# Expert stage of a two-layer model: program order on TensorE, nineteen weight places, another order of gathering

## The chip, the cores and the metric

One core of one Trainium2 chip runs the whole kernel. The metric is device microseconds (us) of one execution, the median of several runs. The engines that matter here are TensorE (PE in the profile, its weight loads PEld), VectorE (DVE), ScalarE (ACT), and SyncE (SP), which issues the weight transfers.

## What is computed

The program is a two-layer model on 512 tokens of 1024 features. The change lies in its last part, a mixture of experts. A router gives every token to experts, each of 16 experts takes its first 64 tokens, and each expert is a gated network whose result is added back to the tokens it took, weighted by the router's share:

```python
def expert(x, w_gate, w_up, w_down):          # x: 64 tokens x 1024
    return (silu(x @ w_gate) * (x @ w_up)) @ w_down
```

So 16 experts times three 1024x1024 float32 matrices, 201 MB in all, are read once and used once.

## The kernel before

Function moe (L1495) works on the experts in NB = 8 pairs, the two experts of a pair in the two halves (64 columns each) of the tiles. A matrix of a pair comes as 8 chunks of 1 MB, 192 chunks in all, in the order in which they are used: gate 0, up 0, then for each later pair b gate b, down b-1, up b, and at the end the down matrix of the last pair ("last").

- **Places for weights.** load (L1512) puts chunk n into place n % 17: 8 tiles e_raw, 4 halves of the tiles xh and xl, 2 tiles wraw, and 3 pairs whi and wlo, of an earlier stage. SyncE issues the transfers in this order. Seventeen chunks are asked for before the first product; from then on chunk (L1630) asks for the next one when it is used, and the transfer waits until TensorE has left the place.
- **gather(b)** (L1590). VectorE makes the selection matrix e_oh and its scaled copy e_ohr (L1595, L1598). TensorE multiplies the tokens e_ht by it (L1605) into two PSUM banks "sm" of four blocks each; a block is 128 features, f = 0 to 7, and each is 4 matmuls of the program (8 instructions in the trace). After each two blocks of a bank they are evicted into e_x, the even one by VectorE (L1614), the odd one by ScalarE (L1612). Then come 4 transposes of e_oh (L1618), copied to e_oht (L1620), and 4 small matmuls for the router's shares (L1623, 8 instructions in the trace).
- **product** (L1636) runs over 8 chunks, 4 matmuls of the program to a chunk, 8 in the trace (L1643), into two banks "mm".
- **turn_hidden** (L1647) transposes the hidden values e_hs (L1653) and copies them to e_hid (L1654). **weigh** (L1664) multiplies the down product by the router's shares into e_y. **spread_out** (L1657) multiplies e_y by e_oht (L1661, 2 matmuls for each of 8 blocks t) and VectorE adds the result to the tokens (L1662).
- The loop (from L1671) runs, for each pair b: gate b; the rest of the spreads of b-2 and turn_hidden of b-1; the tanh (L1681, L1682); down b-1 and weigh; gather(b+1); up b; the multiplication by up (L1691); the first spreads of b-1. This is the order in which the program is written. On TensorE the instructions go as a scheduler puts them, by what is ready and by its own estimates, so that pieces of gather(b+1) and of the spreads stand among the matmuls of the products. At the end stand the last product (L1714), finish (L1701) and the normalization of the output.

Of the kernel before, what the change touches and what calls it, by code (L numbers as in the profile page):

```python
# [19 lines left out]
D = 1024  # L20
S = 512
NK = D // 128
NT = S // 128
DFF = 2816
WC = 272
NR = 8


class G:
    pass  # L30


def f32(t):
# [164 lines left out]
def bc(ap, shape):  # L198
    return ap.to_broadcast(shape)
# [64 lines left out]
class Side:  # L264


    def __init__(self):
        self.q = []
# [17 lines left out]
def sm(g):  # L286
    return g.ps_s.tile([128, 512], F32, name="sm")
# [1207 lines left out]
def moe(g, I, P, x_out, out):  # L1495
# [84 lines left out]
    while len(loaded) < NR + 9:  # L1580
        load()
    ye = P.tile([128, 2, D], F32R, name="e_y")
# [4 lines left out]
    xe, oht, hid = {}, {}, {}  # L1587
    pj = [slice(0, 64), slice(64, 128)]

    def gather(b):  # L1590
# [7 lines left out]
        nc.vector.tensor_mul(ohr, oh.rearrange("p i j c -> p i (j c)"), bc(rt[:, :, None], [128, NT, 128]))  # L1598
        xe[b] = P.tile([128, NK, 2, 64], F32, name="e_x", bufs=2)
        for q in range(2):  # L1600
            p = sm(g)
            for k in range(4):
                f = 4 * q + k
                for i in range(NT):
                    nc.tensor.matmul(p[:, k * 128:(k + 1) * 128], ht[:, i, f * 128:(f + 1) * 128], ohr[:, i, :],  # L1605
                                     start=(i == 0), stop=(i == NT - 1))
                if k % 2:
                    for f in (f - 1, f):
                        o = xe[b][:, f].rearrange("p j c -> p (j c)")
                        pk = p[:, (f % 4) * 128:(f % 4 + 1) * 128]  # L1610
                        if f % 2:
                            nc.scalar.activation(o, pk, AF.Identity, scale=w[:, f:f + 1], bias=shift[:, f:f + 1])  # L1612
                        else:
                            nc.vector.tensor_scalar(o, pk, w[:, f:f + 1], shift[:, f:f + 1], op0=OP.mult, op1=OP.add)  # L1614

        p = sm(g)
        for i in range(NT):
            nc.tensor.transpose(p[:, i * 128:(i + 1) * 128], oh[:, i].rearrange("p j c -> p (j c)"), g.ident)  # L1618
        oht[b] = P.tile([128, S], F32R, name="e_oht", bufs=2)
        nc.scalar.copy(oht[b], p)  # L1620
        pa = sm(g)
        for i in range(NT):
            nc.tensor.matmul(pa[:, 0:2], oh[:, i].rearrange("p j c -> p (j c)"), aff[:, i, 2 * b:2 * b + 2],  # L1623
                             start=(i == 0), stop=(i == NT - 1))
        for j in range(2):
            nc.vector.tensor_copy(affs[pj[j], b:b + 1], pa[pj[j], j:j + 1])

    used = [0]

# [3 lines left out]
        used[0] += 1  # L1633
        return loaded[used[0] - 1]

    def product(lhs):  # L1636

        ps = [g.ps_m.tile([128, 512], F32, name="mm") for _ in range(2)]
        for k in range(NK):
            raw = chunk()  # L1640
            for h in range(2):
                for j in range(2):
                    nc.tensor.matmul(ps[h][pj[j], :], lhs(k, j), raw[j][:, h * 512:(h + 1) * 512], start=(k == 0),  # L1643
                                     stop=(k == NK - 1), skip_group_check=True)
        return ps

    def turn_hidden(b, hs):  # L1647

        hid[b] = P.tile([128, NK, 2, 64], F32, name="e_hid")
        for q in range(2):  # L1650
            p = sm(g)
            for k in range(4):
                nc.tensor.transpose(p[:, k * 128:(k + 1) * 128], hs[q][:, k * 128:(k + 1) * 128], g.ident)  # L1653
            (nc.scalar.copy if q else nc.vector.tensor_copy)(  # L1654
                hid[b][:, 4 * q:4 * q + 4].rearrange("p k j c -> p (k j c)"), p)

    def spread_out(b, t):  # L1657

        p = sm(g)
        for s in range(2):  # L1660
            nc.tensor.matmul(p, ye[:, s, t * 128:(t + 1) * 128], oht[b], start=(s == 0), stop=(s == 1))  # L1661
        nc.vector.scalar_tensor_tensor(g.x[t], p, g.mod[:, 40 + t:41 + t], g.x[t], op0=OP.mult, op1=OP.add)  # L1662

    def weigh(b, cols, p):  # L1664

        nc.scalar.activation(ye[:, 0, cols], p, AF.Copy, scale=affs[:, b:b + 1])
        nc.vector.scalar_tensor_tensor(ye[:, 1, cols], p, affs[:, b:b + 1], f32(ye[:, 0, cols]), op0=OP.mult,
                                       op1=OP.subtract)

    gather(0)  # L1670
    for b in range(NB):  # L1671

        pg = product(lambda k, j: xe[b][:, k, j, :])
# [4 lines left out]
        hs = [P.tile([128, 512], F32, name="e_hs", bufs=2) for _ in range(2)]  # L1678
        for h in range(2):
            th = P.tile([128, S], F32, name="e_full", bufs=2)  # L1680
            nc.scalar.activation(th, pg[h], AF.Tanh, scale=0.5)  # L1681
            nc.vector.scalar_tensor_tensor(hs[h], th, 1.0, pg[h], op0=OP.add, op1=OP.mult)  # L1682
        if b:
            ps = product(lambda k, j: hid[b - 1][:, k, j, :])
            for h in range(2):
                weigh(b - 1, slice(h * 512, (h + 1) * 512), ps[h])
        if b + 1 < NB:
            gather(b + 1)
        pu = product(lambda k, j: xe[b][:, k, j, :])
        for h in range(2):  # L1690
            nc.vector.tensor_mul(hs[h], hs[h], pu[h])  # L1691
        if b:
            for t in range(4 if b + 1 < NB else 8):
                spread_out(b - 1, t)
    turn_hidden(b, hs)

    acc, sq = stat_tiles(g)
    last = [P.tile([128, S], F32, name="e_full", bufs=2) for _ in range(2)]
# [10 lines left out]
    for t in range(NK):  # L1709
        raw = chunk()  # L1710
        p = sm(g)
        for k in range(NK):
            for j in range(2):
                nc.tensor.matmul(p[pj[j], 0:128], hid[b][:, k, j, :], raw[j][:, k * 128:(k + 1) * 128],  # L1714
                                 start=(k == 0), stop=(k == NK - 1), skip_group_check=True)
# [333 lines left out]
```

## Time and profile before

| | us |
|---|---|
| median of 3 runs | 3054.05 (3049.53 to 3057.12) |
| the profiled execution | 3055.56 |
| its span | 3053.5 |
| from the first gather matmul (2562.87) to the first matmul of the last product (3013.80) | 450.93 |

Starts in the rows are microseconds from the start of the span. "x48" is a count of instructions; a matmul's duration includes its way through the array, so that consecutive ones overlap. Names like sm<-e_ohr,e_ht are the program's: result, arrow, operands. In brackets stand the idle time of the engine before a row and what ended it.

### The profile page before, as it was taken

The page shows a single profiled execution, that of the slowest core. Times are in us where ns is not written, and L with a number is a line of the kernel's source. Part 1 is how long each engine was busy: PE and PEld are TensorE (multiplying, and loading weights), DVE is VectorE, ACT ScalarE, POOL GpSimd, SP SyncE. Part 2 cuts the span into 40 slices and gives each one's busy share as a digit, 9 for nine tenths or more (in the row PEclk, how much of TensorE's full clock was granted, in tenths as well). Part 3 has the DMA queues.
Part 4 walks back from the last instruction along what each step waited for, and adds up shares of the span by engine and source line. Part 5 has one row for each costly group of instructions (what it writes and reads, how often), then busy time and mean ns, then how long its engine had stood idle before and what let it go on. Part 6 is the DMA issues. An engine that isn't in the chain of part 4 may idle for free. (4 is left out here: it accounts for less than half of the span.)

```text
span 3053.5 us, 37758 instructions
## 1 busy us (share of the span) xinstructions
PE 2905.0 (95%) x15232; PEld 2225.9 (73%) x15232; DVE 1636.6 (54%) x2847; ACT 905.5 (30%) x1515; POOL 321.4 (11%) x260
## 2 busy tenths in 40 slices
PE   7999998999999999999999999999998877999998
PEld 6888887877888888888776788888787765444444
DVE  4445457665444598545676666454765643122213
ACT  3222334543222332223354433222342321010002
POOL 0001012110201102011210201201100110000000
PEclk9999999999999999999998999999999978999998
DMA  4432343122332358224421233222323435999996
GB/s 146 126 100 92 104 147 116 52 85 84 97 97 94 113 197 297 99 93 135 128 76 56 93 114 104 84 85 90 114 66 94 116 142 201 394 419 418 418 418 277
DMA packets 293107, 472.03 MB, mean 155 GB/s; under 512 B 45215, under 2 KB 237471, under 8 KB 269508
## 3 DMA queue, kind: packets, MB, share of 16 engines
q1 hardware_dynamic: 290216, 466.28, 43.4%
q10 hardware_dynamic: 2716, 3.34, 0.3%
q8 instruction: 120, 1.97, 0.3%
q14 instruction: 55, 0.45, 0.0%
HBM read 449.90 MB, written 19.67 MB: 154 GB/s over the span
## 5 line engine op out<-in xcount | busy, mean ns | idle before, releaser
L69 PE MATMUL mm<-xh,whi 128*128 128x512 f32 x1952 | 777.0, 400 | 12.0 <-ACT xh L146 8.4
L70 PE MATMUL mm<-xl,whi 128*128 128x512 f32 x1952 | 774.9, 397 | 0.6 <-DVE xl L147 0.6
L71 PE MATMUL mm<-xh,wlo 128*128 128x512 f32 x1952 | 772.5, 396 | 1.7 <-DVE wlo L40 1.7
L39 ACT CAST whi<-wraw 128x1024 fp32r<-128x1024 f32 (+3 forms) x390 | 390.9, 1003 | 1113.8 <-PE mm L70 831.4
L40 DVE TENSOR_TENSOR wlo<-wraw,whi 128x1024 fp32r<-128x1024 f32 (+3 forms) x390 | 501.6, 1286 | 97.5 <-ACT whi L39 90.5
L69 PEld LDWEIGHTS mm<-xh,whi 128*128 128x128 f32 x1952 | 372.5, 191 | 92.2 <-ACT xh L146 9.3
L70 PEld LDWEIGHTS mm<-xl,whi 128*128 128x128 f32 x1952 | 372.9, 191 | 82.0 <-issue 3.8
L71 PEld LDWEIGHTS mm<-xh,wlo 128*128 128x128 f32 x1952 | 372.4, 191 | 80.6 <-DVE wlo L40 3.3
L69 PE MATMUL mm<-hh,whi 128*128 128x512 f32 x704 | 279.4, 397 | 0.0
L70 PE MATMUL mm<-hl,whi 128*128 128x512 f32 x704 | 278.7, 396 | 0.0
L71 PE MATMUL mm<-hh,wlo 128*128 128x512 f32 x704 | 278.4, 395 | 0.0
L192 POOL TENSOR_TENSOR x<-x,dt 128x512 f32<-128x512 f32 x72 | 125.7, 1746 | 859.7 <-DVE dt L191 766.0
L172 DVE TENSOR_TENSOR gs<-mm,rb 128x512 f32<-128x512 f32 x88 | 60.8, 691 | 202.5 <-PE mm L71 198.2
L191 DVE SCALAR_TENSOR_TENSOR dt<-mm,rb 128x512 f32<-128x512 f32 x104 | 71.8, 690 | 179.8 <-PE mm L71 179.8
L177 DVE TENSOR_TENSOR gs<-gs,mm 128x512 f32<-128x512 f32 x88 | 60.4, 686 | 196.9 <-PE mm L71 196.8
L71 PEld LDWEIGHTS mm<-hh,wlo 128*128 128x128 f32 x704 | 132.2, 188 | 31.9
L70 PEld LDWEIGHTS mm<-hl,whi 128*128 128x128 f32 x704 | 132.2, 188 | 31.7 <-DVE hl L40 0.3
L69 PEld LDWEIGHTS mm<-hh,whi 128*128 128x128 f32 x704 | 132.2, 188 | 31.6
L1643 PE MATMUL mm<-e_raw,e_x 128*64 128x512 f32 x504 | 118.9, 598 | 0.0
L238 PE MATMUL mm<-whi,xh 128*128 128x512 f32 (+2 forms) x288 | 104.0, 361 | 0.0
L239 PE MATMUL mm<-wlo,xh 128*128 128x512 f32 (+2 forms) x288 | 100.2, 348 | 0.0
L240 PE MATMUL mm<-whi,xl 128*128 128x512 f32 (+2 forms) x288 | 100.2, 348 | 0.0
(646 smaller groups left out, 3561.6 us busy)
## 6 DMA issues: line engine op xcount, KB each, us to landing
wraw<-ffn_gate SPq DMA_DIRECT2D x44, 1024.0 KB, 5.4
wraw<-ffn_up SPq DMA_DIRECT2D x44, 1024.0 KB, 5.3
wraw<-w_in SPq DMA_DIRECT2D x38, 1024.0 KB, 5.3
e_raw<-e_gate SPq DMA_DIRECT2D x36, 1024.0 KB, 12.6
e_raw<-e_up SPq DMA_DIRECT2D x27, 1024.0 KB, 15.0
e_raw<-e_down SPq DMA_DIRECT2D x25, 1024.0 KB, 14.3
wraw<-ffn_down SPq DMA_DIRECT2D x24, 1024.0 KB, 5.1
mw<-w_mod SPq DMA_DIRECT2D x24, 1024.0 KB, 5.0
```

The source lines that it names most:

```text
L39: g.nc.scalar.copy(hi, src)
L40: g.nc.vector.tensor_sub(lo, src, f32(hi))
L69: g.nc.tensor.matmul(out, lh, rh, start=first and i == 0, stop=False, skip_group_check=not (first and last))
L70: g.nc.tensor.matmul(out, lh, rl, start=False, stop=False, skip_group_check=not (first and last))
L71: g.nc.tensor.matmul(out, ll, rh, start=False, stop=last and i == n - 1, skip_group_check=not (first and last))
L172: nc.vector.tensor_mul(gs, pg, rb)
L191: nc.vector.scalar_tensor_tensor(t, pd, 0.25, rb, op0=OP.mult, op1=OP.mult)
L192: (nc.vector if c0 + nch == sum(groups) else nc.gpsimd).tensor_add(g.x[2 * c + m], g.x[2 * c + m], t)
L238: nc.tensor.matmul(o, xh[:, kk, ts], wh[:, k, :], start=(kk == 0), stop=False)
L239: nc.tensor.matmul(o, xh[:, kk, ts], wl[:, k, :], start=False, stop=False)
L240: nc.tensor.matmul(o, xl[:, kk, ts], wh[:, k, :], start=False, stop=(kk == NK - 1))
L1643: nc.tensor.matmul(ps[h][pj[j], :], lhs(k, j), raw[j][:, h * 512:(h + 1) * 512], start=(k == 0), stop=(k == NK - 1), skip_group_check=True)
```

## The change

- A class InOrder wraps TensorE in moe: each of its instructions from the first gather on is held to the order of the program against the others so held (all of them carry line L41 then).
- Nineteen places instead of seventeen: the tiles e_y and a new tile e_h (which later holds hidden values and their transpose) take the first two chunks; the other seventeen go round as before. In the earlier loop the loads after steps 1, 3 and 5 bring the count to 3, 6 and 10 instead of 2, 5 and 8.
- The selection is a function of its own, select(b), which runs a step earlier than the gather that uses it. gather evicts each block right after its 4 matmuls.
- The first gather stands in turns with the first gate product: four blocks, two chunks, two blocks, two chunks, two blocks, two chunks, transposes and shares, two chunks. The later gathers stand whole between down b-1 and up b.
- turn_hidden stands ahead of the spreads of b-2 instead of behind them, and the hidden values of all pairs share one tile.

```diff
+class InOrder:
+    def __init__(self, tc, engine):
+        self.tc, self.engine = tc, engine
+    def __getattr__(self, name):
+        f = getattr(self.engine, name)
+        return lambda *a, **k: self.tc.keep_in_program_order(f(*a, **k))
...
-        place = n % (NR + 9)
-        if place < NR + 6:
-            if place < NR:
+        place = (n - 2) % (NR + 9)
+        if n < 2 or place < NR + 6:
+            if n < 2:
+                raw = P.tile([128, 2 * D], F32, name=("e_y", "e_h")[n])
+            elif place < NR:
...
-            while len(loaded) < NR * (k + 1) // 6:
+            while len(loaded) < (NR + 2) * (k + 1) // 6:
...
+    pe = InOrder(g.tc, nc.tensor)
...
     def gather(b):
-        for q in range(2):
-            p = sm(g)
-            for k in range(4):
-                f = 4 * q + k
-                for i in range(NT):
-                    nc.tensor.matmul(p[:, k * 128:(k + 1) * 128], ht[:, i, f * 128:(f + 1) * 128], ohr[:, i, :],
-                                     start=(i == 0), stop=(i == NT - 1))
-                if k % 2:
-                    for f in (f - 1, f):
...
+        for f in range(NK):
+            if f % 4 == 0:
+                p = sm(g)
+            pk = p[:, (f % 4) * 128:(f % 4 + 1) * 128]
+            for i in range(NT):
+                pe.matmul(pk, ht[:, i, f * 128:(f + 1) * 128], ohr[:, i, :], start=(i == 0), stop=(i == NT - 1))
+            o = xe[b][:, f].rearrange("p j c -> p (j c)")
+            if f % 2:
+                nc.scalar.activation(o, pk, AF.Identity, scale=w[:, f:f + 1], bias=shift[:, f:f + 1])
+                yield
+            else:
+                nc.vector.tensor_scalar(o, pk, w[:, f:f + 1], shift[:, f:f + 1], op0=OP.mult, op1=OP.add)
...
-    gather(0)
     for b in range(NB):
-        pg = product(lambda k, j: xe[b][:, k, j, :])
+        pg = []
+        gate = product(lambda k, j: xe[b][:, k, j, :], pg)
+        if b == 0:
+            select(0)
+            first = gather(0)
+            step(first)
+            for _ in range(4):
+                step(first)
+                step(gate)
...
+        run(gate)
         if b:
+            turn_hidden()
             for t in range(4 if b > 1 else 8, 8):
                 spread_out(b - 2, t)
-            turn_hidden(b - 1, hs)
```

TensorE around gather(3), before. Here sm_19948 and sm_19969 are the gather's two banks, mm_19882 and mm_19883 the banks of a down product that runs at the same time; a count of 4 is one block.

```order
L1605 MATMUL sm_19948<-e_ohr_19945,e_ht_18925 128x128 x2
L1605 MATMUL sm_19969<-e_ohr_19945,e_ht_18925 128x128 x4
L1643 MATMUL mm_19882<-e_raw_19908,e_hid_19861 64x512 [waits DMAHW4_49]
L1643 MATMUL mm_19882<-e_raw_19908,e_hid_19861 64x512
L1643 MATMUL mm_19883<-e_raw_19908,e_hid_19861 64x512 x2
L1605 MATMUL sm_19948<-e_ohr_19945,e_ht_18925 128x128 [waits Activation_49]
L1605 MATMUL sm_19948<-e_ohr_19945,e_ht_18925 128x128 x5
L1643 MATMUL mm_19882<-e_raw_19914,e_hid_19861 64x512 [waits DMAHW5_49]
L1643 MATMUL mm_19882<-e_raw_19914,e_hid_19861 64x512
L1643 MATMUL mm_19883<-e_raw_19914,e_hid_19861 64x512 x2
L1605 MATMUL sm_19948<-e_ohr_19945,e_ht_18925 128x128 x2
L1605 MATMUL sm_19969<-e_ohr_19945,e_ht_18925 128x128 x4
```

TensorE at gather(3) in the changed kernel; sm_19941 and sm_19962 are its two banks.

```order
L41 MATMUL sm_19941<-e_ohr_19782,e_ht_18925 128x128 [waits DVE_49]
L41 MATMUL sm_19941<-e_ohr_19782,e_ht_18925 128x128 x3
L41 MATMUL sm_19941<-e_ohr_19782,e_ht_18925 128x128 [waits DVE_49]
L41 MATMUL sm_19941<-e_ohr_19782,e_ht_18925 128x128 x3
L41 MATMUL sm_19941<-e_ohr_19782,e_ht_18925 128x128 [waits Activation_49]
L41 MATMUL sm_19941<-e_ohr_19782,e_ht_18925 128x128 x3
L41 MATMUL sm_19941<-e_ohr_19782,e_ht_18925 128x128 [waits DVE_49]
L41 MATMUL sm_19941<-e_ohr_19782,e_ht_18925 128x128 x3
L41 MATMUL sm_19962<-e_ohr_19782,e_ht_18925 128x128 x4
L41 MATMUL sm_19962<-e_ohr_19782,e_ht_18925 128x128 [waits DVE_49]
L41 MATMUL sm_19962<-e_ohr_19782,e_ht_18925 128x128 x3
L41 MATMUL sm_19962<-e_ohr_19782,e_ht_18925 128x128 [waits Activation_49]
```

Before, two to six matmuls of the gather stand between chunks of the product, and a bank waits for an eviction only after each two blocks. In the changed kernel the 32 matmuls stand together, and the second, third and fourth block of each bank wait for VectorE or ScalarE: the eviction of the block ahead.

TensorE at the first gather and the first chunks of gate 0, before (sm_19348 and sm_19369 are the banks of gather(0)).

```order
L1605 MATMUL sm_19348<-e_ohr_19345,e_ht_18925 128x128 [waits DVE_49,Activation_49]
L1605 MATMUL sm_19348<-e_ohr_19345,e_ht_18925 128x128 x7
L1605 MATMUL sm_19369<-e_ohr_19345,e_ht_18925 128x128 x5
L1605 MATMUL sm_19348<-e_ohr_19345,e_ht_18925 128x128 [waits Activation_49]
L1605 MATMUL sm_19348<-e_ohr_19345,e_ht_18925 128x128 x7
L1605 MATMUL sm_19369<-e_ohr_19345,e_ht_18925 128x128 x3
```

The same place in the changed kernel; e_y and e_h hold the first two chunks.

```order
L41 MATMUL sm_19351<-e_ohr_19348,e_ht_18925 128x128 [waits DVE_49,Activation_49]
L41 MATMUL sm_19351<-e_ohr_19348,e_ht_18925 128x128 x3
L41 MATMUL sm_19351<-e_ohr_19348,e_ht_18925 128x128 [waits DVE_49]
L41 MATMUL sm_19351<-e_ohr_19348,e_ht_18925 128x128 x3
L41 MATMUL sm_19351<-e_ohr_19348,e_ht_18925 128x128 [waits Activation_49]
L41 MATMUL sm_19351<-e_ohr_19348,e_ht_18925 128x128 x3
L41 MATMUL sm_19351<-e_ohr_19348,e_ht_18925 128x128 [waits DVE_49]
L41 MATMUL sm_19351<-e_ohr_19348,e_ht_18925 128x128 x3
L41 MATMUL mm_19372<-e_y_18993,e_x_19350 64x512 [waits DMAHW7_49]
L41 MATMUL mm_19372<-e_y_18993,e_x_19350 64x512
L41 MATMUL mm_19373<-e_y_18993,e_x_19350 64x512 x2
L41 MATMUL mm_19372<-e_h_18995,e_x_19350 64x512 [waits DMAHW1_49]
```

The first chunk of the gate product moved from behind the whole gather to behind its first four blocks, and the waits for evictions went from one for each bank to three.

SyncE at the first loads of the experts, before.

```order
L1526 DMA e_raw_18993<-e_gate 128x2048 [waits PE_49,Pool_49]
L1526 DMA e_raw_18995<-e_gate 128x2048
L1526 DMA e_raw_19047<-e_gate 128x2048
L1526 DMA e_raw_19049<-e_gate 128x2048
L1526 DMA e_raw_19051<-e_gate 128x2048 [waits DMAHW4_49]
L1526 DMA e_raw_19139<-e_gate 128x2048 [waits DMAHW5_49]
L1526 DMA e_raw_19141<-e_gate 128x2048 [waits DMAHW6_49]
L1526 DMA e_raw_19143<-e_gate 128x2048 [waits DMAHW7_49]
L1526 DMA wraw_19271<-e_up 128x2048 [waits DMAHW0_49,DVE_49]
L1526 DMA wraw_19273<-e_up 128x2048 [waits DMAHW1_49,DVE_49]
```

SyncE in the changed kernel.

```order
L1540 DMA e_y_18993<-e_gate 128x2048 [waits PE_49,Pool_49]
L1540 DMA e_h_18995<-e_gate 128x2048
L1540 DMA e_raw_18997<-e_gate 128x2048
L1540 DMA e_raw_19049<-e_gate 128x2048
L1540 DMA e_raw_19051<-e_gate 128x2048 [waits DMAHW4_49]
L1540 DMA e_raw_19053<-e_gate 128x2048 [waits DMAHW5_49]
L1540 DMA e_raw_19141<-e_gate 128x2048 [waits DMAHW6_49]
L1540 DMA e_raw_19143<-e_gate 128x2048 [waits DMAHW7_49]
L1540 DMA e_raw_19145<-e_up 128x2048 [waits DMAHW0_49]
L1540 DMA e_raw_19147<-e_up 128x2048 [waits DMAHW1_49]
L1540 DMA wraw_19275<-e_up 128x2048 [waits DMAHW2_49,DVE_49]
L1540 DMA wraw_19277<-e_up 128x2048 [waits DMAHW3_49,DVE_49]
```

The eight e_raw tiles moved two places back, behind e_y and e_h, so that two more chunks are asked for before a place has to come free; the waits for one of the eight transfers in flight (DMAHW4 and on) are as before.

## Rows read from the trace of the kernel before

**Rows 1.** Chain of waits from 2565 us to the end: by line, and one piece.

```profile
by line: PE mm L1643 67.5%; PE sm L1605 13.3%; PE sm L1661 7.0%; PE sm L1714 1.9%; PE sm L1623 1.3%; PE sm L1653 1.3%; PE sm L106 0.9%; DVE x L1721 0.9%; DVE e_hs L1691 0.9%; PE sm L1618 0.7%; POOL x L1706 0.5%; issue 0.5%; DVE x L1662 0.4%
...
2628.00 13.88 PE mm L1643 x64
```

**Rows 2.** Engines by stretch: busy PE, PEld, DVE, ACT, POOL; granted clock, DMA share, GB/s.

```profile
2600.00:2700.00 100.00, 99.91 (x501) 42.70 (x498) 18.06 (x32) 8.27 (x15) 0.00 (x0) 1.00 1.00 406
...
2900.00:3000.00 100.00, 97.81 (x473) 41.71 (x471) 20.84 (x34) 8.51 (x15) 0.00 (x0) 1.00 1.02 419
```

**Rows 3.** Groups of TensorE, 2565 to 3053 us: busy, mean ns, idle before, releasers.

```profile
L1643 PE MATMUL mm<-e_raw,e_x 128*64 128x512 f32 x504 | 118.9, 598 | 0.0
...
L1661 PE MATMUL sm<-e_oht,e_y 128*128 128x512 f32 x128 | 39.5, 429 | 2.2 <-ACT e_y L1666 1.8 <-DVE x L1662 0.4
```

**Rows 4.** What SyncE's queue waited for, 2560 to 3053 us: total, times, longest.

```profile
SPq L1526 <- PE mm L1643: 156.7, 72, 38.7
...
SPq L1526 <- DMA e_raw<-e_down: 28.0, 16, 2.1
```

**Rows 5.** Timeline of SyncE, 2545 to 2610 us: start, duration, what.

```profile
2577.03 10.63 SPq L1526 DMA_DIRECT2D e_raw<-e_gate  x7
...
2600.82 2.04 SPq L1526 DMA_DIRECT2D xh<-e_down  x2
```

**Rows 6.** Timeline of all engines at the first two gathers.

```profile
2562.87 8.06 PE L1605 MATMUL sm<-e_ohr,e_ht 128*128 128x128 f32 x48 [1.93 <-DVE e_ohr L1598]
...
2588.95 5.77 PE L1605 MATMUL sm<-e_ohr,e_ht 128*128 128x128 f32 x48
...
2591.04 0.41 DVE L1614 TENSOR_SCALAR e_x<-sm,nm_w,mod 128x128 f32<-128x128 f32 x1 [0.67 <-PE sm L1605]
2591.48 0.46 ACT L1612 ACTIVATE e_x<-sm,mod,nm_w 128x128 f32<-128x128 f32 x1 [1.83 <-DVE e_x L1614]
...
2594.55 0.60 PE L1618 MATMUL sm<-cst,e_oh 128*128 128x128 f32 x4
...
2595.87 0.65 PE L1643 MATMUL mm<-xh,e_x 128*64 128x512 f32 x2
```

**Rows 7.** Timeline of TensorE, 2995 to 3053 us: the first matmul of the last product.

```profile
3013.80 0.32 PE L1714 MATMUL sm<-whi,e_hid 128*64 128x128 f32 x1
```

**Rows 8.** Timeline of TensorE, 2772 to 2812 us: pieces of a gather within products.

```profile
2790.78 1.61 PE L1605 MATMUL sm<-e_ohr,e_ht 128*128 128x128 f32 x12
...
2794.18 1.61 PE L1605 MATMUL sm<-e_ohr,e_ht 128*128 128x128 f32 x12
...
2800.98 1.38 PE L1605 MATMUL sm<-e_ohr,e_ht 128*128 128x128 f32 x10
...
2804.38 1.83 PE L1605 MATMUL sm<-e_ohr,e_ht 128*128 128x128 f32 x14
```

**Rows 9.** Timeline of TensorE, 2750 to 2772 us: spreads, then a product.

```profile
2768.38 1.75 PE L1661 MATMUL sm<-e_oht,e_y 128*128 128x512 f32 x6
2770.06 1.94 PE L1643 MATMUL mm<-wraw,e_x 128*64 128x512 f32 x8
```

**Rows 10.** Matmuls of L1605, 2588.9 to 2594.5 us: ns shortest, median, longest; first and last start.

```profile
L1605 PE MATMUL sm<-e_ohr,e_ht x48: 275/275/377, 2588.9 to 2594.4; 128*128 128x128 f32 x48
```

**Rows 11.** Timeline of TensorE, 2591.9 to 2592.15 us: three gather matmuls.

```profile
2591.73 0.64 PE L1605 MATMUL sm<-e_ohr,e_ht 128*128 128x128 f32 x3
```

**Rows 12.** Timeline of VectorE, 2641 to 2645 us: the two weighings behind a down product.

```profile
2641.82 1.61 DVE L1667 SCALAR_TENSOR_TENSOR e_y<-mm,e_aff,e_y 128x512 fp32r<-128x512 f32 x2 [12.78 <-ACT e_y L1666]
```

**Rows 13.** Groups of VectorE, 2565 to 3053 us: the adding of the spreads.

```profile
L1662 DVE SCALAR_TENSOR_TENSOR x<-sm,mod,x 128x512 f32<-128x512 f32 x64 | 44.4, 745 | 33.1 <-PE sm L1661 33.0
```

**Rows 14.** Engines by stretch in earlier stages where TensorE pauses often.

```profile
2304.00:2308.00 4.00, 2.12 (x41) 1.76 (x41) 2.09 (x2) 2.96 (x4) 0.00 (x0) 1.00 1.17 250
...
2312.00:2316.00 4.00, 2.54 (x70) 2.26 (x72) 3.66 (x15) 1.29 (x2) 0.00 (x0) 1.00 0.33 125
...
2470.00:2474.00 4.00, 2.23 (x8) 1.44 (x8) 4.00 (x8) 0.00 (x0) 2.62 (x3) 0.50 0.00 0
```

More of the change, by code (lines that the diff above doesn't have):

```diff
@@ L1579, in moe @@
         spare += [t[:, 0:2 * D], t[:, 2 * D:]]
-    while len(loaded) < NR + 9:
+    while len(loaded) < NR + 11:
         load()
-    ye = P.tile([128, 2, D], F32R, name="e_y")
     aff, place = [P.tile([128, NT, 16], F32, name="r_" + n) for n in ("aff", "place")]
@@ L1586, in moe, with select @@
     affs = P.tile([128, NB], F32, name="e_aff")
-    xe, oht, hid = {}, {}, {}
+    pe = InOrder(g.tc, nc.tensor)
+    xe, oht, ohs = {}, {}, {}
     pj = [slice(0, 64), slice(64, 128)]
-    def gather(b):
+    def select(b):
         oh = P.tile([128, NT, 2, 64], F32, name="e_oh")
@@ L1598, in gather @@
         nc.vector.tensor_mul(ohr, oh.rearrange("p i j c -> p i (j c)"), bc(rt[:, :, None], [128, NT, 128]))
+        ohs[b] = oh, ohr
+    def gather(b):
+        oh, ohr = ohs.pop(b)
         xe[b] = P.tile([128, NK, 2, 64], F32, name="e_x", bufs=2)
-        for q in range(2):
-            p = sm(g)
-            for k in range(4):
-                f = 4 * q + k
-                for i in range(NT):
-                    nc.tensor.matmul(p[:, k * 128:(k + 1) * 128], ht[:, i, f * 128:(f + 1) * 128], ohr[:, i, :],
-                                     start=(i == 0), stop=(i == NT - 1))
-                if k % 2:
-                    for f in (f - 1, f):
[L1609 to L1614, printed above, removed]
+        for f in range(NK):
[10 more added lines that the diff above has]
+                nc.vector.tensor_scalar(o, pk, w[:, f:f + 1], shift[:, f:f + 1], op0=OP.mult, op1=OP.add)
         p = sm(g)
         for i in range(NT):
-            nc.tensor.transpose(p[:, i * 128:(i + 1) * 128], oh[:, i].rearrange("p j c -> p (j c)"), g.ident)
+            pe.transpose(p[:, i * 128:(i + 1) * 128], oh[:, i].rearrange("p j c -> p (j c)"), g.ident)
         oht[b] = P.tile([128, S], F32R, name="e_oht", bufs=2)
@@ L1622, in gather @@
         for i in range(NT):
-            nc.tensor.matmul(pa[:, 0:2], oh[:, i].rearrange("p j c -> p (j c)"), aff[:, i, 2 * b:2 * b + 2],
-                             start=(i == 0), stop=(i == NT - 1))
+            pe.matmul(pa[:, 0:2], oh[:, i].rearrange("p j c -> p (j c)"), aff[:, i, 2 * b:2 * b + 2],
+                      start=(i == 0), stop=(i == NT - 1))
         for j in range(2):
             nc.vector.tensor_copy(affs[pj[j], b:b + 1], pa[pj[j], j:j + 1])
+        yield
     used = [0]
@@ L1634, in chunk, with product @@
         return loaded[used[0] - 1]
-    def product(lhs):
-        ps = [g.ps_m.tile([128, 512], F32, name="mm") for _ in range(2)]
+    def product(lhs, ps):
+        ps += [g.ps_m.tile([128, 512], F32, name="mm") for _ in range(2)]
         for k in range(NK):
@@ L1642, in product, with turn_hidden @@
                 for j in range(2):
[L1643 to L1649, printed above, removed]
+                    pe.matmul(ps[h][pj[j], :], lhs(k, j), raw[j][:, h * 512:(h + 1) * 512], start=(k == 0),
+                              stop=(k == NK - 1), skip_group_check=True)
+            if k % 2:
+                yield
+    def turn_hidden():
         for q in range(2):
@@ L1652, in turn_hidden @@
             for k in range(4):
-                nc.tensor.transpose(p[:, k * 128:(k + 1) * 128], hs[q][:, k * 128:(k + 1) * 128], g.ident)
+                pe.transpose(p[:, k * 128:(k + 1) * 128], hs[q][:, k * 128:(k + 1) * 128], g.ident)
             (nc.scalar.copy if q else nc.vector.tensor_copy)(
-                hid[b][:, 4 * q:4 * q + 4].rearrange("p k j c -> p (k j c)"), p)
+                hid[:, 4 * q:4 * q + 4].rearrange("p k j c -> p (k j c)"), p)
     def spread_out(b, t):
@@ L1660, in spread_out @@
         for s in range(2):
-            nc.tensor.matmul(p, ye[:, s, t * 128:(t + 1) * 128], oht[b], start=(s == 0), stop=(s == 1))
+            pe.matmul(p, ye[:, s, t * 128:(t + 1) * 128], oht[b], start=(s == 0), stop=(s == 1))
         nc.vector.scalar_tensor_tensor(g.x[t], p, g.mod[:, 40 + t:41 + t], g.x[t], op0=OP.mult, op1=OP.add)
@@ L1668, in weigh, with run, step @@
                                        op1=OP.subtract)
-    gather(0)
-    for b in range(NB):
-        pg = product(lambda k, j: xe[b][:, k, j, :])
+    def run(gen):
+        for _ in gen:
+            pass
+    def step(gen):
+        next(gen, None)
+    for b in range(NB):
+        pg = []
[7 more added lines that the diff above has]
+                step(gate)
+            select(1)
+            t = P.tile([128, 4, 512], F32, name="e_h")
+            hs, hid = [t[:, 0], t[:, 1]], t[:, 2:4].rearrange("p a (k j c) -> p (a k) j c", k=4, j=2)
+            ye = P.tile([128, 2, D], F32R, name="e_y")
+        run(gate)
         if b:
+            turn_hidden()
             for t in range(4 if b > 1 else 8, 8):
                 spread_out(b - 2, t)
-            turn_hidden(b - 1, hs)
-        hs = [P.tile([128, 512], F32, name="e_hs", bufs=2) for _ in range(2)]
         for h in range(2):
@@ L1683, in moe @@
         if b:
-            ps = product(lambda k, j: hid[b - 1][:, k, j, :])
+            pd = []
+            run(product(lambda k, j: hid[:, k, j, :], pd))
             for h in range(2):
-                weigh(b - 1, slice(h * 512, (h + 1) * 512), ps[h])
+                weigh(b - 1, slice(h * 512, (h + 1) * 512), pd[h])
         if b + 1 < NB:
-            gather(b + 1)
-        pu = product(lambda k, j: xe[b][:, k, j, :])
+            run(gather(b + 1))
+        pu = []
+        run(product(lambda k, j: xe[b][:, k, j, :], pu))
         for h in range(2):
             nc.vector.tensor_mul(hs[h], hs[h], pu[h])
+        if b + 2 < NB:
+            select(b + 2)
         if b:
@@ L1694, in moe @@
                 spread_out(b - 1, t)
-    turn_hidden(b, hs)
+    turn_hidden()
     acc, sq = stat_tiles(g)
@@ L1713, in moe @@
             for j in range(2):
-                nc.tensor.matmul(p[pj[j], 0:128], hid[b][:, k, j, :], raw[j][:, k * 128:(k + 1) * 128],
-                                 start=(k == 0), stop=(k == NK - 1), skip_group_check=True)
+                pe.matmul(p[pj[j], 0:128], hid[:, k, j, :], raw[j][:, k * 128:(k + 1) * 128], start=(k == 0),
+                          stop=(k == NK - 1), skip_group_check=True)
         weigh(b, slice(t * 128, (t + 1) * 128), p[:, 0:128])
```

## The prediction

> **What bounds the kernel now.** I read the chain of waits first, over the stretch of the experts. From 2565 us to the end it runs through TensorE almost alone: products 67.5%, gathers 13.3%, spreads 7.0% [rows 1]. Then the engines by stretch: between 2600 and 3000 us TensorE is busy 97.8 to 99.9 us in every 100, at a granted clock of 1.00 (the upper level, 2.4 GHz), and the transfers fill the DMA engines too, 1.00 to 1.02 at 406 to 419 GB/s [rows 2]. Two full resources: which one sets the end? The groups of TensorE tell: it was idle 0.0 us before the largest group of product matmuls, and before the spreads it waited for ScalarE and VectorE, 2.2 us in all [rows 3]. No product matmul waited for a weight. SyncE's queue on the other hand waited 156.7 us, 72 times, for product matmuls to leave a place [rows 4]; its first refills start at 2577.03, and after one more the queue stands until 2600.82, because gather and turn matmuls free no place [rows 5]. So TensorE's queue sets the end, and the transfers follow closely behind it: a chunk of 1024 KB at 419 GB/s takes 2.50 us, 24 of a pair 60.1.
>
> **The stretch that the change touches** goes from the first gather matmul at 2562.87 [rows 6] to the first matmul of the last product at 3013.80 [rows 7]: 450.9 us. What lies behind it is left as it is, and so is all ahead of it: TensorE's instructions up to the first gather stand in the same order in both kernels. The eight first loads, which the router's weights have to share the transfers with, also start as before. I cost these at nothing.
>
> **The work in it, if nothing interrupted it.**
> - 23 products. One that stood in one piece took 13.88 us for 64 instructions [rows 1]: 319.2.
> - 8 gathers of 64 instructions. Pieces of 10 and 14 took 1.38 and 1.83 [rows 8], so each instruction adds 0.1125 us: 7.2 a gather, 57.6.
> - Transposes and shares behind a gather, 2594.55 to 2595.87 [rows 6]: 1.32, times 8 is 10.6.
> - The hidden values: 8 transposes of the gather's shape a pair, 0.9, times 8 is 7.2.
> - Spreads: 6 in the 1.68 from 2768.38 to 2770.06 [rows 9], so 0.28 each; 16 a pair, 7 pairs ahead of the last product: 31.4.
>
> The sum is 426.0. The kernel before needs 24.9 more: interruptions, few waits, and the first gather at the lower clock. What an interruption costs is seen where gather pieces of 12 alternate with product pieces of 8: 3.40 us from one to the next [rows 8], where 12 times 0.1125 and an eighth of 13.88 make 3.09. So 0.31 for going there and back. Program order takes nearly all of these away, since products and gathers then stand whole. That is the change's gain.
>
> **What program order adds.** In the new gather a block is evicted as soon as it is done, and the next block of the same bank waits for that eviction: 3 waits a bank, 6 a gather, 48 in all. The scheduler used to put the other bank or product matmuls there; now nothing else may go. One of the 48 is covered, in the first gather, where two chunks of the product stand ahead of it. What a wait costs:
> - The last matmul of the block is on its way for 0.275 [rows 10].
> - The eviction starts. The sixteenth of the 48 matmuls from 2588.95 starts 15 times 0.1125 later, at 2590.64, and is through at 2590.91; VectorE starts at 2591.04 [rows 6]: 0.13.
> - The eviction takes 0.41 on VectorE, 0.46 on ScalarE [rows 6].
> - TensorE starts again. A block that waited for the ScalarE eviction, over at 2591.94 [rows 6], has its first matmul as the third of three that end at 2592.37 [rows 11]; that one took 0.377 [rows 10], so it started at 2591.99: 0.05.
> - It took 0.10 longer than the others, and the wait contains one usual step of 0.11, which comes off.
>
> Together 0.275 + 0.13 + 0.41 + 0.05 + 0.10 - 0.11 = 0.86, and 47 of them 40.4 us. My bounds for one are 0.70 (no delay at the start of the eviction, no slow first matmul) and 1.0 (all of it, and ScalarE's longer eviction with a late start), so 33 to 47; I take 0.86, since each of its terms stands in a row of the same operation.
>
> **Smaller terms of the order.** Behind a down product VectorE has the two weighings ahead of the first eviction of the next gather: they take 1.61 from the product's end [rows 12], the block is through after about 1.3, so 0.3 for 6 gathers, 1.8. VectorE adds a spread in 0.745 [rows 13] where TensorE makes it in 0.56, with four banks between them: for the four behind each up product and the four behind the hidden values I take 0.3 a pair for five pairs, 1.5; for the last pair's eight, and the hidden copy queued behind them, 2.5. With no spreads to cover it, pair 1's hidden copy costs 0.6. Together 6, bounds 3 and 10. The first 48 gather matmuls took 8.06 where the later ones took 5.77 [rows 6]: 2.3 for the lower clock, which stays in about this size: 2.
>
> **Sum.** 426.0 + 40.4 + 6 + 2 = 474.4 against 450.9: 23.5 slower. The profiled execution took 3055.56, so 3079.1 for it; it stands 1.5 above the median, so **3077.5 us**. Per pair that is about 61.5 of TensorE against 60.1 of transfers: the transfers cease to be full. The two added places move them earlier, to no effect at the end: the places bring weights that TensorE is later still to use.
>
> **The clock** is the term that could be larger. In the new gathers TensorE pauses for about 0.86 us after each 0.9 us. Where it did much the same in an earlier stage, with 2.12 and 2.54 us busy of 4, the granted clock stayed at 1.00; at 2470 us, with 2.23 of 4, it was 0.50 and stayed there, after a stretch of rest [rows 14]. I take no fall, by the first, since TensorE comes from a full product.
>
> The Trainium skill, page "TensorE: Matmul & The Clock Gate", section "A second HAM failure mode: psum-queue depth-cycling", says that a matmul kernel which idled briefly between groups as it cycled through its PSUM banks went back and forth between the two clock levels and lost throughput. That speaks against this change, and the first of the two rows against the rule.
>
> **Rivals.**
> 1. *The clock falls in each gather.* At the lower clock a matmul adds 0.21 instead of 0.11 ((8.06 less 24 at 0.1125 and 0.28 of way) over 24) [rows 6]. If half a gather runs so, that is 32 times 0.1, 3.2 us, and getting back may cost what the first gather lost until its clock rose, 2.3: 5.5 for 7 gathers, 38 more, 3116. For it: the last row of [rows 14]. Against: the first two. Chance 0.12.
> 2. *The waits are cheap, and the transfers set the end: not slower.* If a wait cost under (24.9 - 8) / 47 = 0.36 us, the gain of the order would outweigh it. Then a pair is under 60 us of TensorE and the transfers bound it. Of these, two chunks fewer wait for a place (2 times 2.50), and the restart at 2600.82 comes some 2.6 earlier with the earlier gate product: 7.6 earlier, 3046.5. For it: the transfers are at 1.02 now. Against: the eviction alone takes 0.41, and it would have to cost all of the wait. Much of the gap to my forecast is filled if part of the waits are covered: with half of them, 3057. Chance 0.15.
> 3. *The change does not hold the order.* Then the time would stay at 3054. The listing of the changed kernel shows whole gathers and whole products, so I give it nothing beyond what rival 2 has.
>
> **How the numbers follow.** The forecast has 0.73, and its own range by the bounds of the terms is 3066 to 3090. About 0.3%, 9.2 us, is what a measurement of this kernel tells from no change: faster means below 3044.9, slower above 3063.2. Rival 2 reaches below 3044.9 only if TensorE also gives up its remaining distance to the transfers: 0.05. Same gets the rest of rival 2, 0.10. Slower is the forecast and rival 1: 0.85. The range for 8 in 10 reaches down to the middle of rival 2 and up to the greater part of a falling clock: 3054 to 3106.
>
> **What would show it.** Right: in each gather VectorE and ScalarE evictions one after the other with blocks of 8 matmuls between, TensorE idle some 5 us a gather with those evictions as releasers (about 40 us over the stage), products of 64 in 13.9, the granted clock at 1.00, the DMA share below 1, and the stretch from first gather to last product at 474. Wrong: gathers of 7 to 8 us instead of 12; or a granted clock below 1.00 between 2600 and 3000; or TensorE waiting for a transfer before a product matmul.

## The result, and the profile after

The changed kernel takes 3080.37 us (median of 4 runs, 3079.46 to 3081.54), the kernel before beside it 3055.51: the ratio is 1.0084 (95% interval 1.0069 to 1.0098), 24.9 us slower. 3077.5 was forecast, 23.5 slower; the kernel before itself measured 1.5 above the 3054.05 that the forecast started from. From first gather matmul to last product it is now 475.3 us (2563.76 to 3039.08) against 450.9, where 474.4 was forecast; the stretch ahead is 0.9 longer in this execution, the one behind 0.4 shorter.

Chain of waits after, from 2565 us on; it answers to [rows 1].

```profile
by line: PE mm L41 62.4%; PE sm L41 21.5%; DVE e_x L1630 2.5%; DVE x L1680 2.1%; issue 1.9%; ACT e_x L1627 1.4%; PE sm L117 0.9%; DVE e_h L1719 0.9%; ACT e_y L1684 0.9%; DVE e_y L1685 0.9%; DVE x L1762 0.8%; POOL x L1747 0.5%; PE sm L131 0.
```

TensorE still carries it, but evictions of e_x are now links of the chain: 2.5% on VectorE, 1.4% on ScalarE. Before, TensorE waited for no eviction of e_x at all; the gather's line in its waits from 2560 us on (total, times, longest) was the one ahead of the first gather, and no gather matmul waited for anything else:

```profile
PE sm L1605 <- DVE e_ohr L1598: 1.9, 1, 1.9
```

The same view after, from 2562 us to the last product:

```profile
PE sm L41 <- DVE e_x L1630: 19.6, 32, 0.9
PE sm L41 <- ACT e_x L1627: 8.3, 15, 0.6
...
PE sm L41 <- DVE e_h L1672: 1.3, 1, 1.3
PE mm L41 <- DVE e_h L1672: 0.3, 1, 0.3
```

32 waits for VectorE and 15 for ScalarE: these are the 47 of the prediction, one by one. Timeline of gather(1) after, which answers to [rows 6]:

```profile
2595.86 1.16 PE L41 MATMUL sm<-e_ohr,e_ht 128*128 128x128 f32 x8
...
2597.21 0.41 DVE L1630 TENSOR_SCALAR e_x<-sm,nm_w,mod 128x128 f32<-128x128 f32 x1
...
2597.68 1.16 PE L41 MATMUL sm<-e_ohr,e_ht 128*128 128x128 f32 x8 [0.66 <-DVE e_x L1630]
2598.87 0.46 ACT L1627 ACTIVATE e_x<-sm,mod,nm_w 128x128 f32<-128x128 f32 x1 [2.30 <-PE sm L41]
...
2599.38 1.16 PE L41 MATMUL sm<-e_ohr,e_ht 128*128 128x128 f32 x8 [0.55 <-ACT e_x L1627]
2600.65 0.41 DVE L1630 TENSOR_SCALAR e_x<-sm,nm_w,mod 128x128 f32<-128x128 f32 x1 [3.03 <-PE sm L41]
...
2601.12 2.05 PE L41 MATMUL sm<-e_ohr,e_ht 128*128 128x128 f32 x16 [0.57 <-DVE e_x L1630]
...
2603.68 1.16 PE L41 MATMUL sm<-e_ohr,e_ht 128*128 128x128 f32 x8 [0.51 <-DVE e_x L1630]
```

Eight matmuls, an eviction, eight matmuls: blocks start at 2597.68, 2599.38, 2601.12. Eight instructions without a pause take 0.90, so the wait for ScalarE costs 0.80 and that for VectorE 0.84. The fourth and fifth block follow without a pause, since the fifth starts the second bank; from 2601.12 to 2603.68 that leaves 0.76 for the wait of the sixth. The first product behind such a gather stands whole, as program order wants it, 64 instructions to 2863.10:

```profile
2849.22 13.95 PE L41 MATMUL mm<-e_raw,e_x 128*64 128x512 f32 x64
2863.10 2.32 PE L41 MATMUL sm<-e_oht,e_y 128*128 128x512 f32 x8
```

Engines by stretch after, beside [rows 2]:

```profile
2550.00:2600.00 50.00, 32.89 (x165) 19.92 (x166) 17.41 (x37) 4.09 (x8) 0.00 (x0) 0.74 0.42 161
2600.00:2700.00 100.00, 93.83 (x489) 42.61 (x490) 18.34 (x36) 9.15 (x17) 0.00 (x0) 1.00 0.90 369
2700.00:2800.00 100.00, 92.69 (x488) 43.31 (x486) 19.53 (x38) 8.97 (x17) 0.00 (x0) 1.00 1.02 418
...
2900.00:3000.00 100.00, 93.89 (x484) 43.18 (x486) 18.99 (x35) 7.12 (x14) 0.00 (x0) 1.00 1.01 411
```

TensorE is busy 93 to 95 in 100 where it was 98 to 100; from 2600 us on its granted clock is 1.00 (2.4 GHz). The transfers, which I expected to fall below full, are full again from 2700 us on.

### The profile page after: what moved, and what is told of

Read it like the earlier page. It is cut to its first block, busy times and chain, and to the rows that moved or that the text cites. A ratio compares the mean times of both kernels' runs of the same rounds, so it can differ in the third digit from the quotient of the medians.

```text
span 3078.4 us, 37771 instructions
## 1 busy us (share of the span) xinstructions
PE 2902.9 (94%) x15232; PEld 2225.5 (72%) x15232; DVE 1631.2 (53%) x2847; ACT 908.3 (30%) x1515; POOL 323.6 (11%) x260
## 5 line engine op out<-in xcount | busy, mean ns | idle before, releaser
L41 PE MATMUL mm<-e_raw,e_x 128*64 128x512 f32 x504 | 111.5, 594 | 0.0
L41 PE MATMUL sm<-e_ohr,e_ht 128*128 128x128 f32 x512 | 75.9, 296 | 29.8 <-DVE e_x L1630 19.6
## 6 DMA issues: line engine op xcount, KB each, us to landing
e_raw<-e_down SPq DMA_DIRECT2D x25, 1024.0 KB, 12.2
```

The costliest lines, as they stand in the source:

```text
L41: return lambda *a, **k: self.tc.keep_in_program_order(f(*a, **k))
```

## The experiments

Each ratio compares with the kernel before, run beside it on the same chip; the code cuts are marked by three dots. The start of the first gather moves by several us between executions, so the part from first gather to last product ("the part", from the profile) is compared beside the times.

### Without the waits: a bank for each block

```diff
-            if f % 4 == 0:
-                p = sm(g)
-            pk = p[:, (f % 4) * 128:(f % 4 + 1) * 128]
+            pk = sm(g)[:, 0:128]
```

> The changed kernel, but each of the eight blocks of a gather goes into a PSUM bank of its own, so that no block waits for the eviction of the one ahead. Theory (waits): the 47 waits of 0.83 us are the loss, so TensorE's part from first gather to last product falls from 475.3 us by 39 to about 436. A pair is then under the 60.1 us that its transfers take, and these set the end: they run without a gap from about 2601 us, 165 chunks of 2.50 us to about 3014; the time is 3038 to 3048 us. Rival (the loss lies in the order itself, in products and gathers that no longer overlap): 3070 us or more. Rival (the clock fell later because of the pauses in the first gather): about 4 us of the gain lie in the first gather alone.

Measured: 3051.65 us, ratio 1.0001 (0.9992 to 1.0011), the part 449.3. The order, the places and the evictions are those of the changed kernel, but blocks go through the four "sm" banks in turn; 26 us of its loss are gone with the sharing of banks, which excludes the order itself as the cause. The wait is on a semaphore that the program holds between a block and the eviction of other columns of its bank; whether a kernel could do without it in a shared bank is not tried here. But the time stopped some 4 us above the range that I gave. Timeline of TensorE there, at gather(1) and in the last up product:

```profile
2590.41 7.41 PE L41 MATMUL sm<-e_ohr,e_ht 128*128 128x128 f32 x64
2597.65 0.60 PE L41 MATMUL sm<-cst,e_oh 128*128 128x128 f32 x4
...
3000.16 1.94 PE L41 MATMUL mm<-xh,e_x 128*64 128x512 f32 x8 [0.56 <-DMA xh<-e_up]
3002.64 1.94 PE L41 MATMUL mm<-xl,e_x 128*64 128x512 f32 x8 [0.54 <-DMA xl<-e_up]
3005.13 1.94 PE L41 MATMUL mm<-xl,e_x 128*64 128x512 f32 x8 [0.56 <-DMA xl<-e_up]
```

The gather stands in one piece. In the last pair each chunk now waits 0.54 to 0.56 us for its transfer, and chunks follow at 2.49 us. Chain of waits:

```profile
by line: PE mm L41 41.2%; PE sm L41 17.0%; DMA e_raw<-e_down 6.9%; DMA wraw<-e_gate 4.1%; DMA xl<-e_gate 4.1%; DMA xl<-e_up 4.1%; DMA wraw<-e_down 4.1%; DMA e_raw<-e_gate 3.6%; DMA e_raw<-e_up 3.4%; DMA whi<-e_down 2.8%; DVE x L1678 2.1%; i
```

About a third of the chain is transfers. So the bound that rival 2 named is there as soon as the waits are gone, and it lies about where the kernel before already stood.

### Half the waits: evictions after each two blocks

```diff
-            o = xe[b][:, f].rearrange("p j c -> p (j c)")
             if f % 2:
-                nc.scalar.activation(o, pk, AF.Identity, scale=w[:, f:f + 1], bias=shift[:, f:f + 1])
+                for e in (f - 1, f):
+                    o = xe[b][:, e].rearrange("p j c -> p (j c)")
+                    pk = p[:, (e % 4) * 128:(e % 4 + 1) * 128]
+                    if e % 2:
+                        nc.scalar.activation(o, pk, AF.Identity, scale=w[:, e:e + 1], bias=shift[:, e:e + 1])
+                    else:
+                        nc.vector.tensor_scalar(o, pk, w[:, e:e + 1], shift[:, e:e + 1], op0=OP.mult, op1=OP.add)
                 yield
-            else:
-                nc.vector.tensor_scalar(o, pk, w[:, f:f + 1], shift[:, f:f + 1], op0=OP.mult, op1=OP.add)
```

> The changed kernel, but blocks are evicted after each two, as before. Theory (waits): one wait a bank, for two evictions one after the other: 0.275 + 0.13 + 0.41 + 0.03 + 0.46 + 0.05 + 0.10 - 0.11 = 1.35 us, 15 of them uncovered, 20 us in place of 39: about 3061 us, TensorE's part 456. Rival (order itself): as the changed kernel, 3080 us.

Measured: 3054.75 us, ratio 1.0007 (0.9997 to 1.0016), the part 451.3. TensorE's waits:

```profile
PE sm L41 <- ACT e_x L1630: 14.9, 15, 1.0
```

15 waits of 0.99, as expected in number; with their other parts (0.28 + 0.10 - 0.11) 1.26 each, 19 us. The part is still 4 us below what that gives, and the time 6 below the 3061 expected. About 3 of the 4 lie ahead of gather(1), where the clock rose 2.9 us after the first gather matmul, earlier than in any other run (last section). So that part of this gain is not shown to come from the waits, and the rest of the 4 stays open.

### The places

Seventeen places and the early loads of before, in the changed kernel:

```diff
-        place = (n - 2) % (NR + 9)
-        if n < 2 or place < NR + 6:
-            if n < 2:
-                raw = P.tile([128, 2 * D], F32, name=("e_y", "e_h")[n])
-            elif place < NR:
+        place = n % (NR + 9)
+        if place < NR + 6:
+            if place < NR:
...
-            while len(loaded) < (NR + 2) * (k + 1) // 6:
+            while len(loaded) < NR * (k + 1) // 6:
...
-    while len(loaded) < NR + 11:
+    while len(loaded) < NR + 9:
```

> The changed kernel with the 17 places and the early loads of the kernel before. Theory (TensorE's queue sets the end): 3080 us, within 4 us. Rival (transfers set the end): two more chunks have to wait for a place, 5 us or more longer, 3085 to 3089 us.

Measured: 3076.15 us, ratio 1.0076 (1.0059 to 1.0092), the part 475.4. And nineteen places in the kernel before: the same lines the other way round, and the tile e_h that they need:

```diff
...
-        hs = [P.tile([128, 512], F32, name="e_hs", bufs=2) for _ in range(2)]
+        if b == 0:
+            t = P.tile([128, 4, 512], F32, name="e_h")
+            hs, hid = [t[:, 0], t[:, 1]], t[:, 2:4].rearrange("p a (k j c) -> p (a k) j c", k=4, j=2)
+            ye = P.tile([128, 2, D], F32R, name="e_y")
...
```

> The kernel before with the 19 places, the early loads of 3, 6 and 10 and the shared tile of hidden values, and nothing else of the change. Theory (TensorE's queue sets the end): no change, 3054 us within 4 us, also in the part from first gather to last product (450.9 us). Rival (transfers set the end before): 5 to 7.6 us shorter, 3046 to 3049 us. The scheduler may set another order in other stages, so the part from first gather to last product is compared too.

Measured: 3050.55 us, ratio 0.9995 (0.9985 to 1.0004), the part 449.2. Two places more or fewer change nothing that can be told from no change, in either kernel.

### The order free again

```diff
-    pe = InOrder(g.tc, nc.tensor)
+    pe = nc.tensor
```

> The changed kernel without the program order on TensorE, all else as changed: each block still evicted by itself in a shared bank. Theory (the waits cost because nothing may fill them): the scheduler puts product matmuls and the other bank there, TensorE's idle time before gather matmuls is under 5 us in place of 27.9, and the time is 3050 to 3060 us. Rival (evicting each block by itself costs as such): 3070 us or more.

Measured: 3062.28 us, ratio 1.0017 (1.0008 to 1.0027), the part 459.3; the time is 2 us above the range that I gave. TensorE's waits there:

```profile
PE sm L1624 <- DVE e_x L1630: 1.2, 2, 0.6
```

The scheduler fills all but 1.2 us of the 27.9 (19.6 + 8.3) of the changed kernel, and pays for it with interruptions: TensorE changes between kinds of work (product, gather, transposes and shares, hidden, spread) 180 times in the part, against 143 in the kernel before and 62 in program order. The 37 changes more than before, at the 0.155 each of [rows 8], are 5.7 us; with the waits 6.9 of the 8.4 by which the part is longer. Its rows bear this out as to the place: counted from each row's start to the next, products take 4.9 us more than before and gathers 3.8. That the changes of work are the cause is an estimate and wasn't tried by itself.

### The clock in the first gather

```diff
-            if f % 4 == 0:
+            if f % 4 == 0 or b == 0:
                 p = sm(g)
```

> The changed kernel, with banks of their own for the blocks of the first gather alone. Theory (its pauses also hold the clock back): the granted clock rises 5.2 us after the first gather matmul, as in the kernel before, in place of 11.8; from first gather to last product 469.1 us in place of 475.3: five waits less (three of 0.88 at the lower clock, two of 0.8, together 4.2) and 2.0 for the clock (1.0 in the gather, 1.0 in the first chunk, 1.77 in place of 2.74). Rival (the clock rises as late as in the changed kernel): 471.1 us.

Measured (one run): 3064.8 us, the part 469.0. By stretch, the changed kernel and then this one, from just ahead of the first gather matmul:

```profile
2563.70:2568.00 4.30, 3.73 (x16) 3.47 (x16) 0.41 (x1) 0.00 (x0) 0.00 (x0) 0.50 0.02 4
2568.00:2573.00 5.00, 3.87 (x16) 3.28 (x16) 0.41 (x1) 0.46 (x1) 0.00 (x0) 0.50 0.00 0
2573.00:2576.00 3.00, 3.00 (x12) 1.23 (x12) 0.00 (x0) 0.46 (x1) 0.00 (x0) 0.57 0.00 0
2576.00:2580.00 4.00, 3.49 (x21) 1.63 (x18) 0.41 (x1) 0.00 (x0) 0.00 (x0) 1.00 0.00 0
```

```profile
2555.70:2560.70 5.00, 4.93 (x23) 4.96 (x24) 0.41 (x1) 0.46 (x1) 0.00 (x0) 0.50 0.01 3
2560.70:2565.00 4.30, 4.30 (x27) 2.15 (x26) 0.41 (x1) 0.46 (x1) 0.00 (x0) 0.99 0.00 0
```

Without pauses the granted clock rises from 0.50 (1.2 GHz) to full 5.0 us after the first matmul, as in the kernel before (5.2). With a pause of 0.51 to 0.58 us behind each block it stays at 0.50 for 11.8 us, through the four blocks and into the first chunk. The part is 6.3 us shorter, of which 2.0 were to be the clock; a rise as late as in the changed kernel would have given 471.1.

### Where the transfers set the end: the start

```diff
-        if b + 1 < NB:
+        if b and b + 1 < NB:
             run(gather(b + 1))
         pu = []
         run(product(lambda k, j: xe[b][:, k, j, :], pu))
+        if b == 0:
+            run(gather(1))
```

With banks of their own (on e1):

> e1_own_banks, but gather(1) stands behind up 0 instead of ahead of it. In e1_own_banks TensorE waits for weights (about 11 us in all), and the DMA engines stand idle for 16% of 2580 to 2600 and 21% of 2600 to 2610 us, 5.3 us, because gather(1) frees no place. Theory (without the waits the transfers set the end, and what counts is when places come free at the start): up to 5.3 us shorter than e1_own_banks, 3046 to 3048 us. Rival (TensorE's work sets the end there): 3052 us as before.

Measured: 3048.44 us, ratio 0.9981 (0.9971 to 0.9990), just above the range that I gave; the part 443.2: 6.1 shorter than e1. By stretch, e1 and then this one:

```profile
2580.00:2600.00 20.00, 20.00 (x142) 14.23 (x144) 5.99 (x16) 4.63 (x9) 0.00 (x0) 1.00 0.84 312
2600.00:2610.00 10.00, 10.00 (x50) 3.33 (x48) 0.87 (x2) 0.00 (x0) 0.00 (x0) 1.00 0.79 304
```

```profile
2580.00:2600.00 20.00, 20.00 (x104) 8.20 (x103) 4.51 (x9) 1.78 (x3) 0.00 (x0) 1.00 0.99 396
2600.00:2610.00 10.00, 10.00 (x80) 8.28 (x81) 3.40 (x9) 2.40 (x5) 0.00 (x0) 1.00 1.02 422
```

The gap in the transfers (0.84, 0.79 of the DMA engines) is closed (0.99, 1.02). The same move in the changed kernel, with shared banks:

> The changed kernel with gather(1) behind up 0, its banks shared as changed. This move won 6 us of the part from first gather to last product where no block waits (e1 to f1, by the profile). Theory (in the changed kernel TensorE's own queue sets the end, not the transfers): no change here, 475.3 us within 1.5 in that part, 3078 to 3082 us. Rival (the transfers set the end here too): 469 us, 3074 us.

Measured: 3077.73 us, ratio 1.0079 (1.0064 to 1.0094), the part 475.0. The move did its work on the transfers here too: their share is 0.90 from 2580 to 2600 and 1.02 from 2600 to 2610, against 0.73 and 0.19 in the changed kernel. A move that is worth 6 us where transfers set the end is worth nothing where TensorE's pauses do. This pair says which resource bounds which kernel.

On f1, the places that take one chunk only hold chunks 7 and 8 instead of 0 and 1:

```diff
-        place = (n - 2) % (NR + 9)
-        if n < 2 or place < NR + 6:
-            if n < 2:
-                raw = P.tile([128, 2 * D], F32, name=("e_y", "e_h")[n])
+        place = (n - (n > 7) - (n > 8)) % (NR + 9)
+        if n in (7, 8) or place < NR + 6:
+            if n in (7, 8):
+                raw = P.tile([128, 2 * D], F32, name=("e_h", "e_y")[n - 7])
...
```

> f1_up_before_gather, and the two places that take one chunk only hold the eighth and ninth chunk instead of the first two, so that the first refill comes when chunk 0 is used, at about 2572.5 us instead of 2578.3. Theory (transfers set the end): 5 to 6 us shorter again, 3040 to 3043 us, with TensorE's waits for weights nearly gone; there its own work (449.3 less 11.8 us of waits, 437.5) becomes the limit, so not below 3038. Rival (no effect of when the first place is free): as f1_up_before_gather.

Measured: 3048.93 us, ratio 0.9980 (0.9969 to 0.9991), the part 442.7: no further gain, a miss. The first refill did come with chunk 0, but what it won was lost a little later:

```profile
2560.00:2580.00 20.00, 20.00 (x110) 12.63 (x111) 1.64 (x4) 1.83 (x4) 0.00 (x0) 0.88 0.51 169
...
2600.00:2610.00 10.00, 10.00 (x82) 8.58 (x83) 3.47 (x10) 2.40 (x5) 0.00 (x0) 1.00 0.86 360
```

The transfers run at 0.51 instead of f1's 0.31 up to 2580, and at 0.86 instead of 1.02 from 2600 to 2610: while gather(1) runs, nothing becomes free (SyncE issues nothing from 2599.7 to 2609.8), and the transfers stop because all nineteen places are full. A head start can't be kept beyond the places.

### The best version

On f1, spreads of the last pair but one are put between the chunks of the last up product, where TensorE waits anyway:

```diff
-        run(product(lambda k, j: xe[b][:, k, j, :], pu))
+        up = product(lambda k, j: xe[b][:, k, j, :], pu)
+        if b + 1 == NB:
+            for t in range(4):
+                step(up)
+                spread_out(b - 1, t)
+        run(up)
...
-            for t in range(4 if b + 1 < NB else 8):
+            for t in range(4) if b + 1 < NB else (4, 5):
                 spread_out(b - 1, t)
     turn_hidden()
+    for t in (6, 7):
+        spread_out(b - 1, t)
```

> f1_up_before_gather, with the eight spreads of the last but one pair no longer all behind the last up product: four stand between its chunks, two behind it, two behind the transposes of the hidden values. In f1 TensorE waits about 0.56 us for each of the last chunks, since the transfers take 2.49 and the product 1.75 to 1.9. Theory (transfers set the end up to the last up product, TensorE's queue behind it): four spreads of 0.57 and the wait of 1.3 for the hidden copy leave the path: 3 to 4 us shorter than f1, 3044 to 3046 us. Rival: spreads between the chunks delay the freeing of places: no gain.

Measured: 3045.60 us, ratio 0.9971 (0.9962 to 0.9980): 0.3% below the kernel before, and the lowest median of all. In the trace three of the eight spreads stand between the chunks, three behind the last chunk and two behind the transposes of the hidden values. Behind the last chunk of the last up product, f1 and then this one:

```profile
2993.95 1.94 PE L41 MATMUL mm<-xl,e_x 128*64 128x512 f32 x8 [0.55 <-DMA xl<-e_up]
2995.82 4.30 PE L41 MATMUL sm<-e_oht,e_y 128*128 128x512 f32 x16
3000.04 1.31 PE L41 MATMUL sm<-cst,e_h 128*128 128x128 f32 x8
3002.61 3.60 PE L41 MATMUL sm<-wraw,e_h 128*64 128x128 f32 x62 [1.26 <-DVE e_h L1670]
```

```profile
3001.70 1.94 PE L41 MATMUL mm<-xl,e_x 128*64 128x512 f32 x8 [0.51 <-DMA xl<-e_up]
3003.57 1.66 PE L41 MATMUL sm<-e_oht,e_y 128*128 128x512 f32 x6
...
3006.83 0.73 PE L41 MATMUL sm<-e_oht,e_y 128*128 128x512 f32 x2 [0.26 <-ACT e_h L1670]
3007.50 3.71 PE L41 MATMUL sm<-wraw,e_h 128*64 128x128 f32 x64
```

From that chunk to the last product it is 8.7 us in f1 and 5.8 here, and the wait of 1.26 for the hidden copy has shrunk to 0.26. The part, 442.6, shows 0.6 of this 2.9 only, since up to that chunk this execution is 2.3 behind f1: 0.7 came about ahead of the last down product's final chunks, and about 1.5 at one transfer of the last up product that came late (TensorE waited 1.43 for it). One profile doesn't tell whether that was chance or the spread put ahead of it. The two intervals overlap, and each was measured beside other runs of the kernel before: that i1 beats f1 isn't shown.

## Why the prediction was right

- **The bound.** TensorE's queue, not the transfers, set the end before, and still does after: e3, e4 and h1 move places and transfers and change nothing; e1 takes away TensorE's pauses and wins 26 us.
- **The waits.** 47 of 0.86 were put at 40.4; measured are 16 of 0.84 and 16 of 0.76 for VectorE and 15 of 0.80 for ScalarE, by the three of gather(1), and without what the weighings add to the first wait (below): 37.6. The count was exact, because the order of the changed kernel lists each wait; the size was near because each piece of it stood in a row [rows 6, 10, 11].
- **The gain of the order.** TensorE's part, counted by kind of work from each row's start to the next, is after 102.4 us of gathers, 320.5 of products, 10.6 of transposes and shares and 41.8 of hidden values and spreads; the sum has 101.8, 319.2, 10.6 and 42.8 for these. Before it was 66.2, 331.1, 10.7 and 42.9. So whole products give back 10.6 us, and the loss lies in the gathers alone. In e1 gathers take 60.9 and products 335.9, with 22 waits for weights in them; with the 320.5 of the changed kernel in their place 433.9 would remain, against 426.0 + 6 + 2 = 434 in the sum.
- **Smaller terms.** Behind the weighings TensorE's idle time in the first wait of a gather is 0.81 to 0.89, where the same wait in the second bank has 0.51 (0.3 was taken), and the hidden copies cost 1.3 and 0.3. Waits and smaller terms together come out some 3 us below what I took. The lower clock was under-sized: I took 2, as in the kernel before, and missed that the same pauses hold it back; g1, one run, puts that at 2.0 more. The rest is made up by small excesses, such as 1.3 in the products. So the mechanism and the main terms were right, but that the sum came within 1 us is in part luck: errors of a few us cancel. (The bounds of the terms add up to 3067 to 3088, a little inside the 3066 to 3090 put down.)
- **Rival 1, a falling clock,** did not come: at full clock, gathers of 0.9 us of work and 0.5 to 0.9 of idle kept 1.00, as the first of [rows 14] had it. The rule of the Trainium skill ("TensorE: Matmul & The Clock Gate", section "A second HAM failure mode: psum-queue depth-cycling") did not show itself between 2600 and 3000 us. At the lower clock the same pauses delayed the rise, as the last of [rows 14] had hinted. I weighed the two rows against one another; they stand for two states.
- **Rival 2, the transfers,** failed on its condition: a wait costs 0.76 to 0.84, not under 0.36. It was right about what lies behind the waits: e1 and f1 show chunks at 2.49 us. Its price was wrong: I had it at 3046.5 with the earlier gate product, but e1 took 3051.65, and the transfers have a gap during gather(1) there; f1, which closes the gap, took 3048.44.
- **A miss on the way.** I expected the transfers to cease to be full; they are at 1.01 to 1.02 from 2700 us on. I read this as catching up: after the slow start (0.42 of the DMA engines in 2550 to 2600, 0.19 in 2600 to 2610) many places are free. No run shows that step by step; h1 shows that an earlier start of the transfers wins nothing. A full resource need not be the bound.

## What to carry to other kernels

Before holding an engine to program order, count the waits that the order then exposes: each wait on an eviction in the same PSUM bank cost TensorE 0.8 us here, 47 of them 38 us, and a bank for each block took them all away. When two resources are both nearly full, removing one engine's pauses gains only down to the other's line (3080 to 3052); the next gain lay in keeping that other one from standing still at the start (6 us of the part). And compare a move in both versions: what gains in one and nothing in the other tells which resource bounds.

## What was not expected of the hardware

Pauses of 0.51 to 0.58 us (0.81 to 0.89 for the first of most gathers) between blocks of 8 matmuls left the granted clock at 1.00 once it was there, over gathers of some 12 us, but kept it at 0.50 where it had not yet risen: it rose 11.6 to 12.2 us after the first gather matmul in the three runs with these pauses in the first four blocks (the changed kernel, e3 and h1), and after 4.8 to 5.4 in eight without them. e2 is the exception: it rose after 2.9, ahead of the only pause of that gather, 0.99 us behind its second block. So pauses alone don't decide the moment, and what does isn't settled by these runs.
